# Attention matmuls in a fixed order of one-form blocks, and conditioning in four column groups summed by way of DRAM

## The chip, the core and the metric

The kernel runs on one core of a Trainium2 chip. TensorE (PE) multiplies, VectorE (DVE) and ScalarE (ACT) do the elementwise work, GpSimd (POOL) and SyncE (SP) issue transfers. The metric is the device time of one execution in microseconds, the median of several runs. Every time below comes from the profile, the runs or the trace of this kernel.

## What is computed

Two transformer blocks in sequence on 512 tokens of width 1024, float32. The first block conditions its input on a vector, attends over a neighbourhood and a context, mixes with a gated unit, and ends in a mixture of 16 experts; the second block has two layers. The change touches the first block's conditioning and attention:

```python
def _adaln(cond, w, b):
    return jnp.split(jax.nn.silu(cond) @ w + b, N_MOD, axis=-1)

# first block
sh_a, sc_a, g_a, sh_f, sc_f, g_f = _adaln(c, w_ada[i], b_ada[i])
csh_a, csc_a, ... = _adaln(c_ctx, w_ada[i], b_ada[i])
h = _modulate(x, sh_a[:, None], sc_a[:, None])
q, k, v, u, vs = _project(h, w_in[i], q_gain[i], k_gain[i])
o_na = _neighborhood_attention(q, k, v, kc, vc, rpb[i])   # softmax(q k + bias) v, 8 heads of 64
o_sg = _sgu(u, vs, sgu_ln[i], sgu_w[i], sgu_b[i])         # gelu(u) * (w_s . layernorm(gelu(vs)) + b_s)
x = x + g_a[:, None] * _merge(o_na, o_sg, out_gain[i], w_out[i])
hf = _modulate(x, sh_f[:, None], sc_f[:, None])
x = x + g_f[:, None] * _hier_moe(hf, ...)
```

## The kernel before

The program is written with a planner: it gets instructions with priorities, and itself fixes their order on each engine and the waits between engines. Most products use a split of the operands into a high and a low part and three matmuls (`mm3`, lines 195 to 197); the attention's transposes and value products and all of the conditioning are plain float32, where each 512-column matmul is two records in the trace.

**Conditioning.** `w_ada` is 1024 x 6144, cut into twelve chunks of 512 columns, each two loads of 1 MB. `ada_row` (line 247) multiplies a chunk: eight matmuls, one for each 128 rows of the weight, whose stationary operand `cst` is 64 columns wide (two of them are the two conditions, the rest zero). Even and odd ones write to rows 0 to 63 and 64 to 127 of one PSUM tile (line 263), so a chunk leaves two partial sums. The copy `row` (line 265) goes on to another matmul that adds the two. For the first four chunks, ahead of the projections, that is line 336, which also turns the row into columns (scale and shift of the attention's input). For the other eight, `ada_store` (line 269) adds the partial sums and the bias with a matmul of one output column (`adab`, line 274) and stores the row in `ada_dram`; the rest of the block reads it back as four broadcasts (`g_a`, `sh_f`, `sc_f`, `g_f`, line 835).

**Attention.** In `first_attention` (line 314), after the projections of q, k, v, vs and u, sixteen steps (m, t): four pairs of heads by four tiles of 128 queries. `scores` (from line 486) makes twelve matmuls of 64 rows, two heads side by side, into two PSUM tiles `sc`; DVE adds the bias and takes the maximum (line 503), ACT takes the exponent (line 227 is the helper), DVE the reciprocal and the scaling (line 512). `values` transposes the probabilities (line 522, eight transposes), copies the first head's with ACT and the second's with DVE (lines 525, 527), and makes eight matmuls with 64 columns (line 531) into `o`. Scores run two steps ahead of values. `sgu_norm`, `sgu_mix` and the eight stores stand in a list `fill`; one of them is put into two steps of three. `sgu_out` (the gate's four transposed tiles) comes at step 13. PSUM has four buffers for scores, two for transposes, one for `o` and one, `any`, for all else. `tc.high_priority` gives scores and values a priority, and the planner puts the matmuls of the fill between them as it sees room. After the steps, the squares of the attention's output are summed (line 578), the rows are normalised, and `first_rest` (line 824) makes the output projection, the gate's half of the rows first.

Of the kernel before, what the change touches and what calls it, by code (L numbers as in the profile page):

```python
# [14 lines left out]
P = 128  # L15
# [3 lines left out]
ND = 512  # L19
# [19 lines left out]
C_SEL = 640  # L39
# [229 lines left out]
def ada_store(c, cst, j, dst):  # L269

    nc = c.nc
    row = ada_row(c, cst, j, c.a["b_ada"][j - 4:j - 3, :])
    ps = c.ps("adab")
    nc.tensor.matmul(ps[0:1, :], c.k[0:97, C_SEL:C_SEL + 1], row[0:97, :], start=True, stop=True)
    out = c.t("adao")
    nc.scalar.copy(out[0:1, :], ps[0:1, :])
    nc.gpsimd.dma_start(dst, out[0:1, :])
# [36 lines left out]
def first_attention(c, x, cst, v_dram, ada_dram):  # L314

    nc, tc, a = c.nc, c.tc, c.a
    with ExitStack() as st:
# [13 lines left out]
        with tc.tile_pool(name="early", bufs=6, reuse_waits="tile") as early, tc.issue_after(xload.ins):  # L331
            c.more_raws((early, "raw", 6), own_first=True)
            for j in range(4):
                row = ada_row(c, cst, j)
                for q in range(4):
                    nc.tensor.matmul(pc[:, (j * 4 + q) * 2:(j * 4 + q) * 2 + 2], row[0:66, q * P:(q + 1) * P],
                                     c.k[0:66, C_SEL2:C_SEL2 + 2], start=True, stop=True)
# [119 lines left out]
        def sgu_mix():  # L457
            sgw = R3.tile([P, 8, P], F32, name="sgw", tag="b8")
            nc.gpsimd.dma_start(sgw, a["sgu_w"])
            for g in range(8):  # L460
                po = c.ps("mix")[:, :256].rearrange("p (n d) -> p n d", n=4)
                nc.tensor.matmul(po, sgw[:, g], vn[:, :, g * 64:(g + 1) * 64], start=True, stop=True)
                go = gate[:, :, g * 64:(g + 1) * 64]
                nc.vector.scalar_tensor_tensor(go, po, c.vecs[:, 10 + g:11 + g], go, op0=OP.add, op1=OP.mult)
            ss = R.tile([P, 4], F32, name="ss")
# [4 lines left out]
            for i in range(4):  # L470
                nc.vector.tensor_scalar_mul(gate[:, i], gate[:, i], ss[:, i:i + 1])

        def sgu_out():
            held["y1"] = [c.xs.tile([P, 4, 512], F32R, name="y1", tag="xs") for _ in range(2)]
            for m in range(4):
                ps = c.ps("gT")
                for i in range(4):
                    nc.tensor.transpose(ps[:, i * P:(i + 1) * P], gate[:, i, m * P:(m + 1) * P], c.ident)
                y = c.t("ysg")
                nc.vector.tensor_scalar_mul(y, ps, og[:, 4 + m:5 + m])  # L480
                c.split(held["y1"][0][:, m], held["y1"][1][:, m], y)

        store = lambda j: ada_store(c, cst, j, ada_dram[j - 4:j - 3, :])
        on = []

        def scores(m, t):
            w = WIN0[t]
            sc = [c.ps("sc") for _ in range(2)]
            for part in range(2):
                for step in range(3):  # L490
                    for e in range(2):
# [6 lines left out]
                        nc.tensor.matmul(sc[e][:, part * 256:part * 256 + 256], q, k, start=step == 0, stop=step == 2)  # L498
# [16 lines left out]
        def values(m, t, prob):  # L515
            if t == 0:
                held["o"] = c.ps("o")
            pt = []
            for e in range(2):
                pT = c.ps("pT")  # L520
                for j in range(4):
                    nc.tensor.transpose(pT[:, j * P:(j + 1) * P], prob[e][:, j * P:(j + 1) * P], c.ident)
                pt.append(c.t("pt"))
                if e == 0:
                    nc.scalar.copy(pt[e], pT)
                else:
                    nc.vector.tensor_copy(pt[e], pT)
            for j in range(4):
                v = vw[:, t, j] if j < 2 else vc[:, j - 2]
                for e in range(2):  # L530
                    nc.tensor.matmul(held["o"][e * 64:e * 64 + 64, t * P:(t + 1) * P], v[:, m * P + e * 64:m * P + e * 64 + 64],
                                     pt[e][:, j * P:(j + 1) * P], start=j == 0, stop=j == 3)
            if t == 3:
                on.append(RQ.tile([P, S], F32, name="on", tag="q"))
                nc.scalar.copy(on[m].rearrange("p (r t c) -> p t r c", r=8, t=4),
                               held["o"].rearrange("p (t r c) -> p t r c", t=4, r=8))

# [36 lines left out]
        msq = c.ps("msq")  # L574
        for m in range(4):
# [1015 lines left out]
```

## Time and profile before

| what | us |
|---|---|
| median of three runs (2596.69 to 2597.25) | 2596.92 |
| the profiled execution | 2599.29 |
| its span | 2597.5 |
| PE busy in the span | 2493.9 (96%) |
| DVE busy | 1414.4 (54%) |
| ACT busy | 1058.5 (41%) |

The profile shows one execution. A timeline row has start, duration, engine, line, operation, tiles (out<-in), the array's rows*columns in use, the shape and, in brackets, idle time of the engine before it. A duration has the matmul's way through the array in it, so successive starts tell the pace. A group row has count, busy time, mean duration and the idle time before. The granted clock is a share of 2.4 GHz.

### The profile page before, as it was taken

How to read it: one execution, taken by the hardware profiler on the slowest of the kernel's cores; microseconds unless marked ns; L12 is line 12 of the kernel's file. 1: busy time of each engine (PE TensorE's matmuls, PEld its weight loads, DVE VectorE, ACT ScalarE, POOL GpSimd, SP SyncE). 2: the span in 40 equal slices, each digit the busy share in tenths (PEclk: the TensorE clock that was granted, in tenths of full speed). 3: DMA queues.
4: the chain of work that ended last, by engine and by line, in shares of the span. 5: the costliest groups of instructions: out<-in, count | busy, mean ns of one | idle time of the engine just before them, and what ended most of it. 6: DMA issues, size and time to landing. Idle time of an engine off the chain costs nothing.

```text
span 2597.5 us, 30968 instructions
## 1 busy us (share of the span) xinstructions
PE 2493.9 (96%) x12305; PEld 2024.4 (78%) x12305; DVE 1414.4 (54%) x2393; ACT 1058.5 (41%) x1632; POOL 90.2 (3%) x111
## 2 busy tenths in 40 slices
PE   7999986999999999999999999999999999999997
PEld 3785455888888888887788888888888877888886
DVE  3735355999963333369963333443333699633334
ACT  3523232888842222254652232342222546522222
POOL 0011001121100000000000000000000000000000
PEclk9999987999999999999999999999999999999999
DMA  6243365999932222331122222322222311222231
GB/s 259 82 126 122 130 245 215 358 396 391 389 129 83 97 97 85 105 118 70 66 69 96 98 92 89 110 97 96 94 89 96 118 65 66 82 98 98 77 105 61
DMA packets 59524, 347.98 MB, mean 134 GB/s; under 512 B 8832, under 2 KB 11040, under 8 KB 23280
## 3 DMA queue, kind: packets, MB, share of 16 engines
q1 hardware_dynamic: 47776, 311.45, 32.8%
q0 software_dynamic: 10448, 31.86, 4.2%
q10 hardware_dynamic: 1152, 2.66, 0.3%
q8 instruction: 97, 1.59, 0.3%
q14 instruction: 51, 0.42, 0.0%
HBM read 329.67 MB, written 16.27 MB: 133 GB/s over the span
## 4 chain that ended last, share of the span: by engine, by line
PE 70%; DVE 9%; ACT 4%; issue 1%; ACTq 0%; another core or an unknown queue 0%; DVEq 0%
PE t L195 12%; PE t L196 12%; PE t L197 12%; PE y L195 7%; PE y L197 7%; PE y L196 7%; PE e L195 2%; PE e L197 2%; PE e L196 2%; DVE acc L1222 2%; DVE wl L187 1%; PE ft L195 1%; PE ft L196 1%; PE ft L197 1%; ACT x L1085 1%
## 5 line engine op out<-in xcount | busy, mean ns | idle before, releaser
L186 ACT CAST wh<-raw 128x1024 fp32r<-128x1024 f32 (+1 forms) x504 | 521.5, 1038 | 1077.1 <-PE t L197 350.3
L187 DVE TENSOR_TENSOR wl<-raw,wh 128x1024 fp32r<-128x1024 f32 (+1 forms) x504 | 600.9, 1207 | 605.9 <-ACT wh L186 601.9
L195 PE MATMUL t<-xh,wl 128*128 128x512 f32 x1440 | 562.0, 390 | 0.0
L196 PE MATMUL t<-xl,wh 128*128 128x512 f32 x1440 | 561.2, 390 | 0.0
L197 PE MATMUL t<-xh,wh 128*128 128x512 f32 x1440 | 560.9, 389 | 0.0
L195 PEld LDWEIGHTS t<-xh,wl 128*128 128x128 f32 x1440 | 270.7, 188 | 58.5 <-issue 2.3
L197 PEld LDWEIGHTS t<-xh,wh 128*128 128x128 f32 x1440 | 270.7, 188 | 56.4
L196 PEld LDWEIGHTS t<-xl,wh 128*128 128x128 f32 x1440 | 270.6, 188 | 56.4 <-issue 0.8
L195 PE MATMUL y<-hh,wl 128*128 128x512 f32 (+1 forms) x792 | 289.8, 366 | 2.1 <-DVE x L1049 2.1
L196 PE MATMUL y<-hl,wh 128*128 128x512 f32 (+1 forms) x792 | 290.2, 366 | 0.0
L197 PE MATMUL y<-hh,wh 128*128 128x512 f32 (+1 forms) x792 | 289.4, 365 | 0.0
L1135 DVE SCALAR_TENSOR_TENSOR s<-s,t 128x512 f32<-128x512 f32 x80 | 55.1, 688 | 254.7 <-PE t L197 254.7
L195 PEld LDWEIGHTS y<-hh,wl 128*128 128x128 f32 x792 | 149.3, 189 | 27.0 <-DVE x L1049 2.9
L196 PEld LDWEIGHTS y<-hl,wh 128*128 128x128 f32 x792 | 149.4, 189 | 24.3
L197 PEld LDWEIGHTS y<-hh,wh 128*128 128x128 f32 x792 | 149.4, 189 | 24.1
L195 PE MATMUL ft<-xh,wl 128*128 128x256 f32 x384 | 104.8, 291 | 8.0 <-ACT xh L1090 6.8
L196 PE MATMUL ft<-xl,wh 128*128 128x256 f32 x384 | 110.4, 292 | 0.7 <-DVE xl L1091 0.7
L195 PE MATMUL e<-wh,hTl 128*128 128x512 f32 x272 | 108.3, 398 | 0.5 <-DVE hTl L187 0.5
L197 PE MATMUL ft<-xh,wh 128*128 128x256 f32 x384 | 108.8, 288 | 0.0
L197 PE MATMUL e<-wh,hTh 128*128 128x512 f32 x272 | 106.6, 392 | 0.0
L196 PE MATMUL e<-wl,hTh 128*128 128x512 f32 x272 | 106.4, 391 | 0.0
L1222 DVE SCALAR_TENSOR_TENSOR acc<-yp,hw,acc 128x512 f32<-128x512 f32 x120 | 85.6, 755 | 0.1
(473 smaller groups left out, 3485.7 us busy)
## 6 DMA issues: line engine op xcount, KB each, us to landing
raw<-in_w_gu SPq DMA_DIRECT2D x88, 1024.0 KB, 4.7
raw<-in_w SPq DMA_DIRECT2D x82, 1024.0 KB, 11.4
raw<-in_w_d SPq DMA_DIRECT2D x32, 1024.0 KB, 4.9
raw<-in_w_ada SPq DMA_DIRECT2D x24, 1024.0 KB, 4.9
pair<-in_w SPq DMA_DIRECT2D x14, 1024.0 KB, 12.5
raw<-in_w_in SPq DMA_DIRECT2D x14, 1024.0 KB, 4.7
raw<-in_w_out SPq DMA_DIRECT2D x12, 1024.0 KB, 4.7
raw<-in_w_d SPq DMA_DIRECT2D x32, 384.0 KB, 3.1
```

The lines of the kernel that those rows point to most:

```text
L186: self.nc.scalar.copy(h, x)
L187: self.nc.vector.tensor_sub(l, x, h.bitcast(F32))
L195: mm(ps, al, bh, start=first, stop=False)
L196: mm(ps, ah, bl, start=False, stop=False)
L197: mm(ps, ah, bh, start=False, stop=last)
L1085: nc.scalar.activation(r, t, AF.Identity, bias=b[:, d:d + 1], scale=g[:, d:d + 1])
L1135: nc.vector.scalar_tensor_tensor(s, s, 0.5, ps[1], op0=OP.mult, op1=OP.mult)
L1222: nc.vector.scalar_tensor_tensor(acc[:, t], yp[:, t, j:j + S], w, acc[:, t], op0=OP.mult, op1=OP.add)
```

## The change

In attention, the matmuls are kept in program order (`pin`). A step is written as: the extra work of the step (mixing in steps 1 to 4, the gate's tiles in 7 to 10, three of four square sums in 14), the transposes, the scores of the step after next, in eight of the steps one conditioning chunk, then the values. Both copies of the transposes are DVE's; the scaling of the probabilities and of the gate is ACT's. The normalisation of the gate goes among the u projections. In conditioning, `cst` is 32 columns wide and a chunk's matmuls write to four groups of 32 rows, so there are four partial sums. For the eight later chunks these are stored in DRAM; after every fourth chunk the sums of four are read back in another layout, added on DVE to the bias and stored again. `sc_f` and `sh_f` change places.

```diff
-def ada_row(c, cst, j, bias=None):
+def ada_row(c, cst, j, pin=lambda i: i):
-    if bias is not None:
-        nc.gpsimd.memset(row[64:128, :], 0.0)
-        nc.gpsimd.dma_start(row[96:97, :], bias)
         w = [c.load(c.a["w_ada"][j, half], 2048) for half in range(2)]
     for half in range(2):
         for k in range(4):
-            g = slice(k % 2 * 64, k % 2 * 64 + 64)
-            nc.tensor.matmul(ps[g, :], cst[:, half * 4 + k], w[half][:, k * 512:(k + 1) * 512],
-                             start=half == 0 and k < 2, stop=half == 1 and k > 1)
-    nc.scalar.copy(row[0:66, :], ps[0:66, :])
+            pin(nc.tensor.matmul(ps[k * 32:k * 32 + 32, :], cst[:, half * 4 + k], w[half][:, k * 512:(k + 1) * 512],
+                                 start=half == 0, stop=half == 1))
+    nc.scalar.copy(row[0:98, :], ps[0:98, :])
...
+class Condition:
+    ORDER = (4, 5, 8, 9, 6, 7, 10, 11)
...
+    def chunk(self, n, pin):
+        c, nc = self.c, self.c.nc
+        row = ada_row(c, self.cst, self.ORDER[n], pin)
+        nc.gpsimd.dma_start(self.sums[n], row[0:97:32, :])
+        if n % 4 == 3:
+            part = n // 4
+            t, out = c.t("sums"), c.t("rows")[0:16, 0:P]
+            nc.gpsimd.dma_start(out, c.a["b_ada"][part])
+            for q in range(4):
+                nc.gpsimd.dma_start(t[q * 4:q * 4 + 4, :].rearrange("q (a p) -> q a p", a=4),
+                                    self.sums[part * 4 + q].rearrange("a (q p) -> q a p", p=P))
+            for a in range(4):
+                nc.vector.tensor_add(out, out, t[0:16, a * P:(a + 1) * P])
+            nc.gpsimd.dma_start(self.dst[part].rearrange("r (q p) -> (r q) p", p=P), out)
...
-        def sgu_mix():
+        def sgu_mix(g2):
...
+            ps = c.ps("mix")
+            for g in range(2 * g2, 2 * g2 + 2):
+                po = ps[:, g % 2 * 256:g % 2 * 256 + 256].rearrange("p (n d) -> p n d", n=4)
+                pin(nc.tensor.matmul(po, held["sgw"][:, g], vn[:, :, g * 64:(g + 1) * 64], start=True, stop=True))
...
-        def sgu_out():
+        def sgu_out(m):
+            ps = c.ps("gT")
+            for i in range(4):
+                pin(nc.tensor.transpose(ps[:, i * P:(i + 1) * P], gate[:, i, m * P:(m + 1) * P], c.ident))
+            h, l = held["y1"][0][:, m], held["y1"][1][:, m]
+            nc.scalar.mul(h, ps, og[:, 4 + m:5 + m])
+            nc.vector.scalar_tensor_tensor(l, ps, og[:, 4 + m:5 + m], h.bitcast(F32), op0=OP.mult, op1=OP.subtract)
...
+        pin = tc.keep_in_program_order
...
             for e in range(2):
-                nc.vector.tensor_scalar_mul(prob[e], prob[e], s8[:, 3, e:e + 1])
+                nc.scalar.mul(prob[e], prob[e], s8[:, 3, e:e + 1])
...
+        def turned(prob):
             pt = []
             for e in range(2):
                 pT = c.ps("pT")
                 for j in range(4):
+                    pin(nc.tensor.transpose(pT[:, j * P:(j + 1) * P], prob[e][:, j * P:(j + 1) * P], c.ident))
                 pt.append(c.t("pt"))
-                if e == 0:
-                    nc.scalar.copy(pt[e], pT)
-                else:
-                    nc.vector.tensor_copy(pt[e], pT)
+                nc.vector.tensor_copy(pt[e], pT)
+            return pt
...
+        def squares(m):
+            if m == 0:
+                held["msq"] = c.ps("msq")
+            sq = c.t("osq")
+            nc.scalar.square(sq, on[m])
+            pin(nc.tensor.matmul(held["msq"], c.ones, sq, start=m == 0, stop=m == 3))
...
         for i in range(4):
             u_tile(i)
+            if i == 1:
+                sgu_norm()
         phase.close()
-        fill = [sgu_norm, sgu_mix] + [lambda j=j: store(j) for j in range(4, 12)]
+        cond = Condition(c, cst, sums_dram, ada_dram)
+        extra = {1 + g: [lambda g=g: sgu_mix(g)] for g in range(4)}
+        extra[5] = [sgu_scale]
+        extra.update({7 + m: [lambda m=m: sgu_out(m)] for m in range(4)})
+        extra[14] = [lambda m=m: squares(m) for m in range(3)]
...
-                if j % 3 != 2 and fill:
-                    fill.pop(0)()
-                if j == 13:
-                    sgu_out()
+                for f in extra.get(j, ()):
+                    f()
+                s, prob = ready.pop(0)
+                pt = turned(prob)
                 if j + 2 < 16:
-                    with tc.high_priority(offset=0):
-                        ready.append((steps[j + 2], scores(*steps[j + 2])))
-                s, prob = ready.pop(0)
-                with tc.high_priority(offset=0):
-                    values(*s, prob)
+                    ready.append((steps[j + 2], scores(*steps[j + 2])))
+                if j in (0, 2, 4, 6, 8, 10, 12, 13):
+                    cond.chunk((j + 1) // 2, pin)
+                values(*s, pt)
+            squares(3)
+            rs = c.t("ors")
+            c.rstd(rs, held["msq"], ND, 1e-6)
...
-        for j, n in enumerate(("g_a", "sh_f", "sc_f", "g_f")):
+        for j, n in enumerate(("g_a", "sc_f", "sh_f", "g_f")):
...
-        cst = first.tile([P, KD, 64], F32, name="cst")
+        cst = first.tile([P, KD, 32], F32, name="cst")
```

## Rows read from the trace of the kernel before

**Rows 1.** Table of stretches: length, busy PE, PEld, DVE, ACT, POOL, clock, DMA, GB/s

```profile
150.00:200.00 50.00, 50.00 (x222) 41.01 (x220) 13.22 (x16) 13.57 (x17) 3.84 (x6) 1.00 0.46 130
...
200.00:210.00 10.00, 7.94 (x57) 6.58 (x57) 8.73 (x28) 5.86 (x13) 0.00 (x0) 0.80 0.00 0
...
270.00:280.00 10.00, 10.00 (x37) 4.06 (x35) 0.83 (x2) 1.64 (x3) 1.51 (x3) 1.00 0.00 0
...
340.00:350.00 10.00, 3.84 (x17) 2.81 (x16) 9.27 (x17) 3.80 (x9) 1.06 (x2) 0.50 0.66 222
```

**Rows 2.** Groups by line and form, 200 to 410 us: busy us, mean ns, idle before

```profile
L263 PE MATMUL ada<-raw,cst 128*64 128x512 f32 x128 | 48.8, 608 | 0.4 <-DVE gate L464 0.3
...
L227 ACT ACTIVATE ring<-sc,s 128x512 f32<-128x512 f32 x32 | 21.7, 681 | 18.0 <-DVE s L505 17.9
L503 DVE CUSTOM_DVE_ANT_1 sc<-sc,bias 128x512 f32<-128x512 f32 x24 | 16.3, 707 | 27.8 <-PE sc L498 27.6
...
L527 DVE COPY pt<-pT 128x512 f32<-128x512 f32 x16 | 11.1, 691 | 58.2 <-PE pT L522 43.6 <-issue 14.6
...
L274 PE MATMUL adab<-row,consts 97*1 97x512 f32 x16 | 8.2, 590 | 0.0
L227 ACT ACTIVATION_READ_ACCUMULATOR ring<-sc,s 128x1 f32 x32 | 6.3, 196 | 0.0
...
L503 DVE DVE_READ_ACCUMULATOR2_ANT s<- 128x1 f32 x32 | 4.6, 142 | 0.0
...
L186 ACT CAST y<-ysg 128x512 fp32r<-128x512 f32 x4 | 2.5, 622 | 5.8 <-DVE ysg L480 5.8
```

**Rows 3.** Timeline of PE, transposes and conditioning in alternation

```profile
245.88 0.33 PE L522 MATMUL pT<-consts,ring 128*128 128x128 f32 x1
246.14 1.07 PE L263 MATMUL ada<-raw,cst 128*64 128x512 f32 x2
247.15 0.33 PE L522 MATMUL pT<-consts,ring 128*128 128x128 f32 x1
```

**Rows 4.** Timeline of PE, unbroken blocks

```profile
227.86 1.09 PE L522 MATMUL pT<-consts,ring 128*128 128x128 f32 x8
...
292.49 3.65 PE L263 MATMUL ada<-raw,cst 128*64 128x512 f32 x16
295.98 0.38 PE L531 MATMUL o<-pt,vw 128*64 128x128 f32 x2
```

**Rows 5.** Timeline of PE, start of the attention steps

```profile
199.93 0.39 PE L498 MATMUL sc<-kh,ql 64*128 64x256 f32 x2
...
200.74 0.28 PE L498 MATMUL sc<-kh,ql 64*128 64x256 f32 x2
...
205.99 1.97 PE L522 MATMUL pT<-consts,ring 128*128 128x128 f32 x8
```

**Rows 6.** Timeline of PE, end of the attention and first output matmul

```profile
355.92 3.70 PE L578 MATMUL msq<-osq,consts 128*128 128x512 f32 x8
362.51 0.50 PE L195 MATMUL wo<-wh,y 128*128 128x512 f32 x1 [2.89 <-DVE rs L211]
```

**Rows 7.** Timeline of PE, conditioning ahead of the projections

```profile
19.29 3.65 PE L263 MATMUL ada<-raw,cst 128*64 128x512 f32 x16
...
35.33 3.66 PE L263 MATMUL ada<-raw,cst 128*64 128x512 f32 x16
39.66 1.05 PE L336 MATMUL cols<-consts,row 66*128 66x2 f32 x8 [0.68 <-ACT row L265]
```

**Rows 8.** The tile of the early weight loads: issues, and time to landing

```profile
L139 SPq DMA_DIRECT2D raw<-in_w_ada x8: 328/376/671, 1.6 to 15.5; - x8
...
DMA to landing us min/median/max: 11.3/12.6/13.4
```

**Rows 9.** Transfers issued 190 to 380 us: count, KB, median us to landing

```profile
raw<-in_w_ada SPq DMA_DIRECT2D x14, 1024.0 KB, 4.7
...
ada_dram<-adao POOLq DMA_DIRECT2D x8, 2.0 KB, 2.2
```

More of the change, by code (lines that the diff above doesn't have):

```diff
@@ L261, in ada_row, with __init__ @@
         for k in range(4):
-            g = slice(k % 2 * 64, k % 2 * 64 + 64)
-            nc.tensor.matmul(ps[g, :], cst[:, half * 4 + k], w[half][:, k * 512:(k + 1) * 512],
-                             start=half == 0 and k < 2, stop=half == 1 and k > 1)
-    nc.scalar.copy(row[0:66, :], ps[0:66, :])
-    return row
[L269 to L277, printed above, removed]
+            pin(nc.tensor.matmul(ps[k * 32:k * 32 + 32, :], cst[:, half * 4 + k], w[half][:, k * 512:(k + 1) * 512],
+                                 start=half == 0, stop=half == 1))
+    nc.scalar.copy(row[0:98, :], ps[0:98, :])
+    return row
+class Condition:
+    ORDER = (4, 5, 8, 9, 6, 7, 10, 11)
+    def __init__(self, c, cst, sums_dram, rows_dram):
+        self.c, self.cst, self.sums, self.dst = c, cst, sums_dram, rows_dram
+    def chunk(self, n, pin):
[12 more added lines that the diff above has]
+            nc.gpsimd.dma_start(self.dst[part].rearrange("r (q p) -> (r q) p", p=P), out)
 def rms_in(c, x, n):
@@ L335, in first_attention @@
                 for q in range(4):
-                    nc.tensor.matmul(pc[:, (j * 4 + q) * 2:(j * 4 + q) * 2 + 2], row[0:66, q * P:(q + 1) * P],
-                                     c.k[0:66, C_SEL2:C_SEL2 + 2], start=True, stop=True)
+                    nc.tensor.matmul(pc[:, (j * 4 + q) * 2:(j * 4 + q) * 2 + 2], row[0:98, q * P:(q + 1) * P],
+                                     c.k[0:98, C_SEL2:C_SEL2 + 2], start=True, stop=True)
             bias = c.vecs[:, V_ADA:V_ADA + 16].unsqueeze(2).to_broadcast([P, 16, 2])
@@ L455, in sgu_norm, with sgu_scale @@
                 nc.vector.tensor_mul(vn[:, i], vn[:, i], lnb)
-        def sgu_mix():
[L458 to L462, printed above, removed]
+        def sgu_mix(g2):
+            if g2 == 0:
+                held["sgw"] = R3.tile([P, 8, P], F32, name="sgw", tag="b8")
+                nc.gpsimd.dma_start(held["sgw"], a["sgu_w"])
+            ps = c.ps("mix")
+            for g in range(2 * g2, 2 * g2 + 2):
+                po = ps[:, g % 2 * 256:g % 2 * 256 + 256].rearrange("p (n d) -> p n d", n=4)
+                pin(nc.tensor.matmul(po, held["sgw"][:, g], vn[:, :, g * 64:(g + 1) * 64], start=True, stop=True))
+            for g in range(2 * g2, 2 * g2 + 2):
+                po = ps[:, g % 2 * 256:g % 2 * 256 + 256].rearrange("p (n d) -> p n d", n=4)
                 go = gate[:, :, g * 64:(g + 1) * 64]
                 nc.vector.scalar_tensor_tensor(go, po, c.vecs[:, 10 + g:11 + g], go, op0=OP.add, op1=OP.mult)
+        def sgu_scale():
             ss = R.tile([P, 4], F32, name="ss")
@@ L470, in sgu_mix @@
             for i in range(4):
-                nc.vector.tensor_scalar_mul(gate[:, i], gate[:, i], ss[:, i:i + 1])
-        def sgu_out():
[L474 to L483, printed above, removed]
+                nc.scalar.mul(gate[:, i], gate[:, i], ss[:, i:i + 1])
+        def sgu_out(m):
+            if m == 0:
+                held["y1"] = [c.xs.tile([P, 4, 512], F32R, name="y1", tag="xs") for _ in range(2)]
+            ps = c.ps("gT")
[5 more added lines that the diff above has]
+        pin = tc.keep_in_program_order
         on = []
@@ L497, in scores @@
                             k = (kch, kcl, kch)[step][pr, m]
-                        nc.tensor.matmul(sc[e][:, part * 256:part * 256 + 256], q, k, start=step == 0, stop=step == 2)
+                        pin(nc.tensor.matmul(sc[e][:, part * 256:part * 256 + 256], q, k, start=step == 0, stop=step == 2))
             s8 = c.cst.tile([P, 4, 2], F32, name="s8", tag="s8", bufs=4)
@@ L530, in values @@
                 for e in range(2):
[L531 to L532 removed]
+                    pin(nc.tensor.matmul(held["o"][e * 64:e * 64 + 64, t * P:(t + 1) * P],
+                                         v[:, m * P + e * 64:m * P + e * 64 + 64],
+                                         pt[e][:, j * P:(j + 1) * P], start=j == 0, stop=j == 3))
             if t == 3:
@@ L1479, in host @@
     b_ada = f("b_ada")[0].reshape(12, 512)[perm]
[L1480 removed]
+    o["b_ada"] = b_ada[list(Condition.ORDER)].reshape(2, 16, P)
     w = f("w_in")[0]
```

31 lines of the change are left out of this document (11 added, 20 removed).

## The prediction

> **What bounds the kernel now.** The busy shares of the page say that TensorE (PE) works nearly all the time, so I went to what fills that time. The table of stretches comes first: in the attention stage PE is busy from end to end (10.00 of 10 us between 270 and 280) while DVE works 0.83 and ACT 1.64 us; near its end PE does 3.84 of 10 us at a granted share of 0.50, which is 1.2 of 2.4 GHz; the start (200 to 210) stands at 0.80 [rows 1]. So PE sets the pace there. Next, whether that work has to cost so much. The timeline shows why not: in the middle of the stage single instructions of different shapes take turns. One transpose and then one conditioning instruction: the transpose goes at 245.88, the conditioning matmul at 246.14, the next transpose at 247.15 [rows 3]. In a block of its own kind the same conditioning work costs far less: 16 records (8 instructions of two) from 292.49 to 295.98, 3.49 us [rows 4], so 0.436 us for an instruction, against 1.01 in the alternation. Two things are lost: 64-column instructions stand side by side in pairs only if they follow each other (one alone takes 0.87), and each turn of shape costs another 0.12 to 0.14 us, which I take as 0.15.
>
> The stage runs from the first score, 199.93 [rows 5], to the first square sum, 355.92 [rows 6]: 156.0 us. In whole blocks its work would be: 8 conditioning chunks x 3.49 = 27.9; 8 bias sums (adab), 8.2 in all [rows 2]; 16 steps of scores at 0.81 (199.93 to 200.74, the next step's first) [rows 5] = 13.0; 16 x 8 transposes at 1.09 [rows 4] = 17.4; 16 value blocks, by an estimate from the chunk's pace (a record of 512 columns 0.218, so of 128 columns 0.055, 16 of them 0.87) = 13.9; the gate's mixing and transposes by the same paces 3.5 + 2.2. Together 86 us. Some 70 us are alternation, waits and the half clock.
>
> **The change, part by part.** *Four column groups.* A chunk keeps 8 matmuls, but four run side by side instead of two. The trace shows that two groups halve the time (3.49 for 8, where one alone costs 0.87). Four are not shown: between no gain (3.49) and a further half (1.74). I take 1.74, because the step from one group to two was whole, and keep 3.49 for the range. The Trainium skill, "TensorE: Matmul & The Clock Gate", section "Measured speedup vs the span model", gives three 32-column tiles as 2.38 times one; carried on to four, an estimate, a chunk would cost 2.2 us and the twelve chunks of the kernel together 5 us more than my sum, and no run here shows it.
>
> *Early conditioning (4 chunks before the projections).* Chunks start at 19.29 and 35.33, three periods of 5.35 us, each 3.49 of matmuls, the rest row copy and column sums; the last sums begin at 39.66 [rows 7]. Less 1.74 each, the fourth chunk would start at 19.29 + 3 x 3.61 = 30.1. Its weights don't hold it up: the last load is issued at 15.5 and lands within 13.4, by 29 [rows 8]. Everything behind follows the column sums: 4 x 1.74 = 7.0 us won, or 0 if four groups are no faster.
>
> *Attention in fixed blocks.* A step is now 8 transposes (1.09), scores of the step after next (0.81 + 0.15), in every second step a chunk (1.74 + 0.15), values (0.87 + 0.15). Sum: 16 x 3.07 = 49.1; 8 x 1.9 = 15.2; mixing 3.5, gate transposes 2.2, three square sums 2.6 (they come before transposes, the same shape). The bias sums leave PE. Total 72.6 us if nothing waits.
>
> *What now waits.* PE's order is fixed, so a late operand holds all that is behind it.
> (1) Start: from the first scores to the first transpose the softmax takes 205.99 - 199.93 = 6.1 us [rows 5]; PE has two score blocks (1.6) and then nothing: 4.4 us. Before, it slipped scores of later steps in there.
> (2) Each step's values wait for both transposes to be copied by DVE, 2 x 0.69 [rows 2], since ACT's copy moves to DVE and the scaling of the probabilities from DVE to ACT. PE has 0.96 of scores to cover 1.4 and perhaps a running reduction (0.71 + 0.14): 0.4 to 1.3 exposed in the 8 steps without a chunk, 0.8 taken, 6.4 us; a chunk covers it in the others.
> (3) One PSUM buffer serves chunks, mixing and gate transposes in turn. In steps 7 to 10 ACT and then DVE empty it in a row (0.62 + 0.7 and their queues); six hand-overs at 1 to 2.5 us, 10 us.
> (4) The chunk of step 13 comes one step after that of 12; a load takes 4.7 us from issue [rows 9] and its buffer comes free only with the former chunk: 3 us.
> (5) Clock: a lull at the start already has the share at 0.80 there [rows 1], and mine is longer: work of about 6 us at half speed, 3 us lost.
> The softmax of a step, 6.1 - 0.8 = 5.3 us, has to fit between its scores and its transposes: values 1.0, transposes 1.1, scores 1.0, a chunk 1.9, values 1.0 make 6.0. It fits, narrowly. DVE needs 2 x 0.85 + 2 x 0.69 = 3.1 us a step, 49 in all; ACT 2 x (0.68 + 0.20) and two scalings, estimated at the 0.62 of an ACT pass of that shape, 3.0 a step, 48 in all, and some 28 passes besides at 0.6, 17 [rows 2]. Both stay under PE's 72.6.
> Stage: 72.6 + 4.4 + 6.4 + 10 + 3 + 3 = 99.4, so 156.0 - 99.4 = 56.6 us won.
>
> *End.* Three of four square sums are made early; output matmuls that need only the gate's half may start behind the last values, where before they waited 6.6 us (355.92 to 362.51) for the normalisation [rows 6]. They have 48 matmuls to cover it. 0.5 us left over: 6.1 won, 0 if their buffers are again those of the square sum.
>
> *Sums by way of DRAM, other moves.* A chunk's four partial rows are stored, read back, added on DVE and stored again: three trips at about 2.2 us [rows 9]; for each half of the rows POOL's queue carries ten instructions, where it had twelve (memset, load and store for each chunk). The first half is complete at step 6, the second at step 13, some 12 us before the stage ends; the second's broadcasts are wanted only after the first output half. Cost 0; if the additions stand at the head of DVE's queue before their data is there, DVE and with it PE waits up to 6 us, twice. The gate's normalisation (eight DVE passes, one broadcast load on POOL's queue, two more loads of ACT's table) goes among the u projections, where in 50 us DVE works 13.22 and ACT 13.57 [rows 1]: 0. On POOL's queue the first half's read-backs stand ahead of the last head pair's bias table (issued at step 8, wanted at 10) and the second half's ahead of the last two broadcasts; both have steps to spare.
>
> Sum: 7.0 + 56.6 + 6.1 = 69.7. The profiled execution took 2599.29 us (span 2597.5), the median of the runs 2596.92, 0.1% apart; I subtract from the median: 2527.
>
> **The rivals.** *Four groups run no faster than two.* Early gain 0; 8 x 1.74 = 13.9 more on PE, of which some 3 fill waits: 2527 + 7 + 11 = 2545. For it: nothing in the trace has four. Against: the whole gain from one to two.
> *The clock stays at 1.2 GHz through the stage*, because PE now rests in every step. 2 x 72.6 + 4.4 = 150 us: 6 won there, 2577 in all. For it: the 0.80 and 0.50 of stretches with lulls [rows 1]. Against: at half speed the work leaves no rests, and full stretches stand at 1.00.
> *Evictions on one engine are the bound.* What the trace shows is that DVE's share of these copies lasts 0.69 us each [rows 2]. If they come behind reductions every time, 0.7 us more is exposed in each step: 16 x 0.7 = 11, 2538. The Trainium skill, "TensorEngine Tiling (Array Packing)", section "PSUM Bottleneck", asks for both engines at this place; the change goes against it.
> *Slower.* The narrow fit fails: softmax of one step no longer runs beside the blocks of others, because DVE's or ACT's queue holds one step's pass behind another's. A step is then 3.07 + 0.95 + 4.4 (chain without scores) + 1.4 (copies) = 9.8 us, 157 in all, and PE, busy 4 of 9.8, falls to 1.2 GHz: 64 more, about 2660 with the rest. It decides from 10.7 us a step, (156 + 13)/16. Against it: 6.0 over 5.3.
> *It doesn't do what it says:* PE's blocks come apart all the same, and the new trips to DRAM cost what is saved: about 2597.
>
> **How the numbers follow.** Forecast 0.66, four groups useless 0.11, low clock 0.08, evictions 0.07, slower 0.05, no effect 0.03. Low end: waits (3) to (5) gone (16 us) and cheaper turns (56 x 0.05 = 3) and some 6 of (2): 2502. High end: the first and third rival together, 2556, and part of the second: 2566. Under 0.2% (5 us) a measurement can't tell from no change; faster 0.92, within it 0.03, slower 0.05.
>
> **What would show it.** Column sums ending at 33 to 35 instead of 40.7; conditioning blocks of about 1.8 us; transposes, scores and values in unbroken blocks; a step of 5 to 6 us; from first score to last value 90 to 110 us; output matmuls within 1 us of the last value; the rest of the kernel unchanged in length. Wrong would be: chunks still 3.5 us, the share of the clock near 0.5 over the stage, PE waiting for DVE's copies by more than 1.5 us a step, DVE waiting for loads from the sums.

## The result, and the profile after

| | before | after |
|---|---|---|
| median, us (4 runs each) | 2597.09 | 2530.78 |
| lowest to highest | 2596.69 to 2597.93 | 2528.66 to 2532.05 |
| span of the profiled execution | 2597.5 | 2529.0 |
| first score to last value, starts, us | 199.93 to 355.72 | 193.06 to 288.71 |
| last column sum, starts | 40.46 | 33.13 |
| first output matmul, starts | 362.51 | 291.30 |
| last output matmul, starts | 419.84 | 351.44 |

The ratio is 0.9742, 95% interval 0.973 to 0.9754: 66 us faster, where 2527 was forecast. The rows below follow the order of the sum. All are of the changed kernel unless a sentence names another.

Stretches (length; busy PE, PEld, DVE, ACT, POOL; granted clock; DMA; GB/s):

```profile
193.00:289.00 96.00, 79.83 (x743) 54.51 (x742) 59.32 (x157) 64.34 (x134) 14.29 (x28) 0.93 0.57 210
193.00:203.00 10.00, 5.91 (x49) 4.61 (x52) 5.25 (x15) 7.33 (x14) 0.00 (x0) 0.76 0.00 0
233.00:243.00 10.00, 8.08 (x73) 5.76 (x70) 3.83 (x14) 8.39 (x19) 1.78 (x4) 0.84 0.56 209
243.00:253.00 10.00, 9.88 (x96) 7.25 (x95) 7.79 (x21) 5.94 (x14) 1.91 (x4) 0.85 0.35 118
289.00:300.00 11.00, 9.68 (x34) 7.19 (x35) 1.81 (x3) 2.53 (x4) 5.64 (x10) 0.84 0.96 390
```

The stage is 96 us, and PE works 79.8 of them. It was 156 with PE busy from end to end in the middle [rows 1]. The share of the clock is 0.93: parts of the stage run at 1.2 instead of 2.4 GHz, the start among them, after a lull.

PE's conditioning group in the stage (busy us, mean ns, idle before and its releaser):

```profile
L258 PE MATMUL ada<-raw,cst 128*32 128x512 f32 x128 | 17.0, 645 | 2.7 <-DMA raw<-in_w_ada 2.5
```

The same 128 records, 17.0 us of PE where there were 48.8 [rows 2].

PE's timeline, first the early chunks, then the first transposes, a step in blocks, and the end of the stage:

```profile
18.86 1.92 PE L258 MATMUL ada<-raw,cst 128*32 128x512 f32 x16
22.47 1.92 PE L258 MATMUL ada<-raw,cst 128*32 128x512 f32 x16
...
32.33 1.05 PE L345 MATMUL cols<-consts,row 98*128 98x2 f32 x8 [0.70 <-ACT row L260]
...
198.84 1.97 PE L535 MATMUL pT<-consts,ring 128*128 128x128 f32 x8 [4.09 <-ACT ring L527]
...
213.72 1.93 PE L258 MATMUL ada<-raw,cst 128*32 128x512 f32 x16
215.57 0.66 PE L546 MATMUL o<-pt,vw 128*64 128x128 f32 x8
...
290.32 1.97 PE L559 MATMUL msq<-osq,consts 128*128 128x512 f32 x2 [1.34 <-ACT osq L558]
291.30 1.41 PE L194 MATMUL wo<-wh,y 128*128 128x512 f32 x1
```

A chunk is now 1.85 us from its start to the next kind of work (213.72 to 215.57), where the block of before took 3.49 [rows 4]; the early chunks follow each other after 3.61 us, not 5.35 [rows 7]. Counted over the whole stage, PE's work turns from one kind to another (conditioning, bias sum, score, value, and transposes with all full-width work) 54 times; in the kernel before it was 240 times.

PE's waits in the stage (us, times, longest):

```profile
PE o L546 <- DVE pt L537: 6.1, 7, 2.0
PE pT L535 <- ACT ring L527: 4.1, 1, 4.1
PE ada L258 <- DMA raw<-in_w_ada: 2.5, 2, 1.4
PE gT L493 <- ACT row L260: 1.9, 1, 1.9
PE mix L473 <- ACT row L260: 1.1, 1, 1.1
```

### The profile page after: what moved, and what is told of

It is laid out like the page before. It is cut to its first block, busy times and chain, and to the rows that moved or that the text cites. A ratio compares the mean times of both kernels' runs of the same rounds, so it can differ in the third digit from the quotient of the medians.

```text
span 2529.0 us, 30912 instructions
## 1 busy us (share of the span) xinstructions
PE 2416.5 (96%) x12289; PEld 1998.9 (79%) x12289; DVE 1405.1 (56%) x2373; ACT 1073.7 (42%) x1650; POOL 89.2 (4%) x107
## 4 chain that ended last, share of the span: by engine, by line
PE 72%; DVE 9%; ACT 4%; issue 1%; DMA 0%; DVEq 0%; another core or an unknown queue 0%; ACTq 0%
PE t L194 12%; PE t L196 12%; PE t L195 12%; PE y L194 7%; PE y L196 7%; PE y L195 7%; PE e L194 2%; PE e L196 2%; PE e L195 2%; DVE acc L1246 2%; DVE wl L186 1%; PE ft L194 1%; PE ft L195 1%; PE ft L196 1%; ACT x L1109 1%
```

## The experiments

Times are medians; each kernel ran beside the kernel before, at 2598.0 to 2599.1 in these runs, so ratios are what is compared. "Stage" is from the start of the first score to that of the last value.

| kernel | us | ratio, 95% interval | stage, us | turns of kind |
|---|---|---|---|---|
| before | 2597.09 | 1 | 155.8 | 240 |
| after | 2530.78 | 0.9742 (0.973, 0.9754) | 95.6 | 54 |
| planner_order: after, no hold in program order | 2520.76 | 0.9704 (0.9688, 0.972) | 85.6 | 83 |
| planner_priority: the same, with the priority of before | 2590.24 | 0.9965 (0.9952, 0.9978) | 161.8 | 303 |
| before_no_priority: before, without the priority | 2565.88 | 0.9878 (0.9863, 0.9893) | 125.2 | 117 |
| before_four_groups: before, four groups | 2578.99 | 0.9931 (0.9914, 0.9947) | 145.2 | 216 |
| before_both: before, both of these | 2558.29 | 0.9848 (0.9832, 0.9865) | 124.7 | 110 |
| two_groups: after, two groups | 2542.66 | 0.9791 (0.9775, 0.9807) | 104.0 | 54 |
| both_copy: after, copies on both engines | 2531.7 | 0.9746 (0.973, 0.9762) | 94.9 | 54 |
| sums_on_pe: after, sums on TensorE | 2538.88 | 0.977 (0.9756, 0.9783) | 111.1 | 62 |
| one_early: after, the 1 added early | 2523.98 | 0.9715 (0.9702, 0.9728) | 95.6 | 54 |
| chunk_first: after, a chunk ahead of the steps | 2524.31 | 0.9711 (0.9698, 0.9724) | 97.6 | 54 |
| both: the last two edits together | 2527.53 | 0.9721 (0.9708, 0.9734) | 97.8 | 54 |
| planner_one: no hold, the 1 added early | 2515.25 | 0.9676 (0.9663, 0.969) | 86.3 | 86 |

### What makes the blocks

**The hold taken away.**

```diff
-        pin = tc.keep_in_program_order
+        pin = lambda i: i
```

> The changed kernel, but the matmuls of the stage are not held in program order; the planner places them. Four groups, sums by way of DRAM and the moves between ACT and DVE stay. If the alternation of shapes is what cost the old stage its 70 us, PE's timeline falls apart again into single instructions and most of the 50 us of the stage return: 2570 to 2585. If the gain is in fewer and better spread operations, under 10 us return: 2531 to 2541.

Measured 2520.76: 10 us faster than with the hold. My theory, that the hold makes the blocks, fell, and the rival's 2531 to 2541 was missed as well. The planner alone leaves 83 turns, not 240, and does better than the fixed order. Which way the 10 us go shows in the stretches of the two stages; of this kernel:

```profile
192.40:278.20 85.80, 81.03 (x743) 52.68 (x742) 56.79 (x151) 63.98 (x134) 14.84 (x29) 1.00 0.60 222
```

PE is busy 81.0 us, 1.2 more than with the hold (79.8), but at full clock, and rests 4.8 us instead of 16.2. With the hold, the granted share of 0.93 means 0.07 x 96 = 6.7 us of full clock withheld. So its work at full clock is some 73 us, 8 less than without it, and it pays 11.4 more in rests and 6.7 in clock. That is how the 10.2 us between the two stages divide.

**The priority put back.** In the kernel before, scores and values stood under a priority (`tc.high_priority`, described with the attention loop ahead of the prediction); the change drops it when it rewrites that loop, and the prediction gave this no term. This kernel has no hold and gives the priority back to transposes, scores and values.

```diff
-        pin = tc.keep_in_program_order
+        pin = lambda i: i
...
-                pt = turned(prob)
+                with tc.high_priority(offset=0):
+                    pt = turned(prob)
                 if j + 2 < 16:
-                    ready.append((steps[j + 2], scores(*steps[j + 2])))
+                    with tc.high_priority(offset=0):
+                        ready.append((steps[j + 2], scores(*steps[j + 2])))
...
-                values(*s, pt)
+                with tc.high_priority(offset=0):
+                    values(*s, pt)
```

> The changed kernel without the hold, and with the priority of the kernel before given to transposes, scores and values (not to chunks, mixing and gate tiles). Theory: in the kernel before it was this priority that put single transposes, score and value matmuls between those of the chunks, since the favoured work takes every free slot and what is not favoured fills the gaps one instruction at a time; then this kernel alternates again: over 150 turns of shape in the stage where the one without hold and priority has 84, the stage 25 to 45 us longer, 2545 to 2565. Rival: the order in which a step is written and the four groups carry the gain, and the priority changes little: 2518 to 2530.

Measured 2590.24, slower than the theory's 2545 to 2565: nearly the whole gain is gone. The stretch of its stage, its conditioning group, and a piece of its timeline:

```profile
194.40:356.50 162.10, 155.62 (x743) 71.31 (x742) 60.42 (x157) 64.32 (x134) 16.07 (x31) 0.98 0.39 136
```

```profile
L258 PE MATMUL ada<-raw,cst 128*32 128x512 f32 x128 | 54.2, 604 | 0.0
```

```profile
255.99 0.33 PE L535 MATMUL pT<-consts,ring 128*128 128x128 f32 x1
256.25 1.04 PE L258 MATMUL ada<-raw,cst 128*32 128x512 f32 x2
257.22 0.33 PE L535 MATMUL pT<-consts,ring 128*128 128x128 f32 x1
257.48 1.04 PE L258 MATMUL ada<-raw,cst 128*32 128x512 f32 x2
```

This is the alternation of before [rows 3], with four column groups in place. PE does the same instructions as the kernel above and needs 155.6 us for them instead of 81.0. It hardly waits (6.5 us), and its clock is granted at 0.98: the loss is in how the work is cut up. The conditioning group alone goes from 18.1 us in planner_order to 54.2, since one conditioning instruction by itself (two records) takes 0.97 us of PE (256.25 to 257.22) with 32 columns, about what it took with 64, 1.01 [rows 3].

**The kernel before without the priority.**

```diff
                 if j + 2 < 16:
-                    with tc.high_priority(offset=0):
-                        ready.append((steps[j + 2], scores(*steps[j + 2])))
+                    ready.append((steps[j + 2], scores(*steps[j + 2])))
                 s, prob = ready.pop(0)
-                with tc.high_priority(offset=0):
-                    values(*s, prob)
+                values(*s, prob)
```

> The kernel before with the priority of scores and values taken away and nothing else. Theory (the priority makes the alternation): the conditioning chunks go in whole blocks, 8 x (8 x 1.01 - 3.49) = 36 us at most come back, some of it is lost to waits since nothing else is reordered: 2560 to 2580, and fewer than 150 turns of shape in the stage. Rival (the written order makes it): within 10 us of the kernel before, 2588 to 2608.

Measured 2565.88, 32.7 less than before in the same runs, within the theory's range. Its stage and its conditioning group:

```profile
198.40:323.80 125.40, 112.91 (x753) 68.25 (x752) 70.19 (x186) 53.82 (x121) 17.55 (x35) 0.90 0.49 177
```

```profile
L263 PE MATMUL ada<-raw,cst 128*64 128x512 f32 x128 | 36.6, 598 | 0.2
```

So two kernels, old writing and new, agree: with the priority PE's work comes apart, without it there are less than half as many turns, and nobody has to hold it. Whether a hold would make the blocks with the priority still in place was not run. What it costs depends on the writing: 33 us in the old, 69 in the new.

### Four column groups

**The changed kernel with two groups**, in the form of the kernel before (64 columns, groups at 0 and 64, two partial sums to store and add).

```diff
-            pin(nc.tensor.matmul(ps[k * 32:k * 32 + 32, :], cst[:, half * 4 + k], w[half][:, k * 512:(k + 1) * 512],
-                                 start=half == 0, stop=half == 1))
+            g = slice(k % 2 * 64, k % 2 * 64 + 64)
+            pin(nc.tensor.matmul(ps[g, :], cst[:, half * 4 + k], w[half][:, k * 512:(k + 1) * 512],
+                                 start=half == 0 and k < 2, stop=half == 1 and k > 1))
...
```

> The changed kernel with two column groups of 64 in place of four of 32 in all twelve chunks; order, sums by way of DRAM and all else as changed. If four groups side by side save what the sum says (1.74 us a chunk), the early chunks lose 7.0 and the stage 8 x 1.74 less what fills waits, 11: 2530.8 + 18 = 2549. If the fixed order alone makes the gain and PE's rests in the stage swallow the longer chunks, the stage loses under 3: 2541.

Measured 2542.66, 12 us above the changed kernel and between the two expectations. The early part loses what it had won (last column sum 39.63, not 33.13), and the stage is 8.4 us longer, not 13.9:

```profile
198.70:302.90 104.20, 88.86 (x743) 59.06 (x742) 58.44 (x153) 64.45 (x134) 15.21 (x30) 0.97 0.54 194
```

PE is busy 9.0 us more and rests 0.9 less. The rests hardly cover the longer chunks: waits for the value operands fall to 3.2 us from 6.1, but those for the gate's and the mixing's buffer grow to 5.7 from 3.0. More than half of what is missing from 13.9 is the clock, granted at 0.97 instead of 0.93, some 3 us withheld instead of 6.7; why it fell less was not tested.

**The kernel before with four groups and no other edit** (the same four lines as in the change, with a 99-row selection for the bias sum).

> The kernel before, with four column groups alone: chunks in four groups, the four partial sums and the bias added by the same one-column matmul. The planner's order stays. The early chunks win 7.0. In the stage, if alternation rules, an instruction that stands alone costs 1.0 us whether 64 or 32 columns wide; only chunks in blocks gain, so 0 to 8 of the possible 14: 2582 to 2590. If the chunk's own work ruled, all 14: 2576. A much larger gain would speak against alternation.

Measured 2578.99, 19.6 less, in between once more. The early part wins 7.4 us and the stage 10.6. Its conditioning group shows why not more, and why not nothing:

```profile
L262 PE MATMUL ada<-raw,cst 128*32 128x512 f32 x128 | 37.4, 603 | 0.5 <-DVE gate L463 0.3
```

48.8 became 37.4: whole blocks are halved, single instructions between others are not.

**Both edits in the kernel before: four groups and no priority.**

> The kernel before with two parts and nothing else: the priority of scores and values taken away, and four column groups for all twelve chunks (bias sums stay on TensorE). Alone the first gave 33 us and the second 19.6 us. Theory: they take different time (turns of shape, and the length of a chunk), the sum is 52.3 and the time 2546, the rest of the change (its other writing, the bias sums off TensorE) is then worth 25 us, down to the 2520.8 of the changed kernel without hold. Rival: four groups pay more in whole blocks, where all 16 records lie side by side (the chunks of the stage took 36.6 us without the priority and take 18.5 in the best kernel, 18 less, and 7 early): 25 us from 2566, so 2541 or below.

Measured 2558.29, and both expectations fell: beside before_no_priority only the early 7 us are won, and the stage does not shrink (124.7 against 125.2).

```profile
192.50:317.40 124.90, 109.89 (x753) 62.11 (x752) 71.55 (x186) 53.18 (x121) 17.66 (x35) 0.88 0.48 178
```

```profile
L262 PE MATMUL ada<-raw,cst 128*32 128x512 f32 x128 | 26.7, 639 | 0.0
L273 PE MATMUL adab<-row,consts 99*1 99x512 f32 x16 | 8.2, 590 | 2.8 <-DMA row<-in_b_ada 1.6 <-ACT row L264 1.2
```

Conditioning takes 9.9 us less of PE (36.6 to 26.7), but PE as a whole is busy only 3.0 less and rests 2.5 more. The scores' groups, laid out anew by the planner, take 4.8 more (45.3 to 50.1 in the sum of their six groups), bias sums wait 1.8 us longer, and the clock is granted at 0.88 instead of 0.90; how much of the 4.8 is the lower clock was not separated. The remaining 39 us between this stage and the 85.6 of planner_order are the rest of the new writing: sums off PE (below), the gate's work ahead of the stage and in pieces, the scaling on ACT. Only the first was tried by itself, in the held order; it made 15.5 us of stage there, so some 24 of the 39 have no part of the change shown for them. One place shows in the trace of before_both:

```profile
295.00:317.40 22.40, 13.93 (x82) 8.88 (x82) 12.89 (x17) 8.67 (x13) 2.10 (x4) 0.70 0.63 247
```

PE rests 8.5 us here, most of them for the gate's transposes, which wait for DVE, and some 6.7 us of clock are withheld. In the changed kernel the gate's tiles stand in steps 7 to 10. That this is what they win was not tested.

### Copies on both engines

**ACT copies the first head's transposes again, and DVE scales the probabilities.**

```diff
                 pt.append(c.t("pt"))
-                nc.vector.tensor_copy(pt[e], pT)
+                if e == 0:
+                    nc.scalar.copy(pt[e], pT)
+                else:
+                    nc.vector.tensor_copy(pt[e], pT)
...
-                nc.scalar.mul(prob[e], prob[e], s8[:, 3, e:e + 1])
+                nc.vector.tensor_scalar_mul(prob[e], prob[e], s8[:, 3, e:e + 1])
```

> The changed kernel, but the transposes of the first head are copied by ACT and those of the second by DVE, and DVE scales the probabilities, as before the change. If two copies in a row on DVE are what PE's values wait for (6.1 us in the changed kernel's trace), most of that goes: 2525 to 2528. If the passes only change engines and the scaling now stands between DVE's reductions, the softmax gets no shorter and the waits move from the values to the transposes: 2529 to 2537.

Measured 2531.7, no difference from the changed kernel. PE's waits in the stage only change their name:

```profile
PE o L549 <- ACT pt L538: 4.2, 5, 2.5
PE pT L535 <- DVE ring L527: 3.4, 1, 3.4
...
PE o L549 <- DVE pt L540: 2.6, 3, 0.9
```

4.2 + 2.6 in the place of 6.1. Both engines serve one chain per step, and moving a pass from one to the other moves the wait with it. A small gain may be hidden: the stage is 0.7 us shorter, but the output matmuls then wait 4.2 us for `y`, not 2.2 (the wait of the next part).

### The sums by way of DRAM

**Sums on TensorE again, in the held order.** Each chunk's four partial rows and the bias are added by a one-column matmul after the step's values, and the row is stored.

```diff
-        nc.gpsimd.dma_start(self.sums[n], row[0:97:32, :])
-        if n % 4 == 3:
...
+    def sum(self, pin):
...
+        ps = c.ps("adab")
+        pin(nc.tensor.matmul(ps[0:1, :], c.k[0:99, C_SEL:C_SEL + 1], self.row[0:99, :], start=True, stop=True))
+        out = c.t("adao")
+        nc.scalar.copy(out[0:1, :], ps[0:1, :])
+        nc.gpsimd.dma_start(self.dst[n // 4][n % 4:n % 4 + 1, :], out[0:1, :])
...
```

> The changed kernel, but the four partial sums of the eight later chunks and the bias are added by a one-column matmul behind the step's values, as in the kernel before; nothing goes by way of DRAM but the finished row. Price by the sum: 8 x (0.87 + 0.15) = 8 us more on PE and a further hand-over of the one PSUM buffer, less the tail's wait for the broadcasts (3 to 5): 2534 to 2540. If the way by DRAM costs more than it saves, this one is faster than 2530.

Measured 2538.88, as expected: the way through DRAM is worth 8 us net. The group says where they are:

```profile
L286 PE MATMUL adab<-row,consts 99*1 99x512 f32 x16 | 8.2, 594 | 9.2 <-ACT row L261 9.2
```

8.2 us of matmuls and 9.2 of waiting for the row's copy; the stage is 15.5 us longer. In the kernel before the same sums waited for nothing [rows 2], so the 9.2 belong to their place right behind the step's values, and another place was not tried. About half comes back after the stage, because the output matmuls are then not held up as follows.

**Where the way through DRAM costs time.** In the changed kernel the first output matmul is 71.2 us earlier than before (362.51 to 291.30), the last only 68.4 (419.84 to 351.44). POOL and then DVE after the last values:

```profile
288.64 0.53 POOL L286 DMA_DIRECT2D ada_dram<-rows  x1 [5.68 <-DVE cum L691]
289.16 0.59 POOL L859 DMA_DIRECT2D g_a<-ada_dram  x1
289.75 0.53 POOL L859 DMA_DIRECT2D sc_f<-ada_dram  x1
```

```profile
302.09 0.69 DVE L860 TENSOR_SCALAR sc_f<-sc_f 128x1024 f32<-128x1024 f32 x1 [6.50 <-DMA sc_f<-ada_dram]
302.70 0.68 DVE L212 TENSOR_TENSOR ors<-rs,rs 128x512 f32<-128x512 f32 x1
303.42 0.75 DVE L607 SCALAR_TENSOR_TENSOR yna<-on,vecs,ors 128x512 f32<-128x512 f32 x1
```

The rows of `sc_f` are complete since the first half, but their broadcast stands on POOL's queue behind the store of the second half, which waits for DVE's additions. It is issued at 289.75 and takes 12.3 us to land. On DVE, `sc_f` plus 1 stands ahead of the attention's normalisation, so that waits 6.5 us for a number that is needed much later. PE has the first half of the output matmuls to do meanwhile and rests 2.2 us ahead of the second:

```profile
306.15 0.50 PE L194 MATMUL wo<-wh,y 128*128 128x512 f32 x1 [2.18 <-DVE y L186]
```

**The 1 added to the 16 rows of sums**, ahead of the additions, so that no DVE pass waits for the broadcast.

```diff
+            if part == 0:
+                nc.vector.tensor_scalar(out, out, c.k[0:16, C_SCF:C_SCF + 1], None, op0=OP.add)
             for a in range(4):
                 nc.vector.tensor_add(out, out, t[0:16, a * P:(a + 1) * P])
...
-        nc.vector.tensor_scalar_add(bcs["sc_f"], bcs["sc_f"], 1.0)
...
```

> The changed kernel, but the one that is added to the scale of the second modulation is added to the 16 x 128 rows of the sums, ahead of the store, and not by DVE to the broadcast. In the changed kernel that pass waits 6.5 us at the head of DVE's queue for the broadcast, and the normalised rows behind it come late: PE rests 2.2 us and works 3.4 us at half the clock. If that is what is lost after the stage, output matmuls run through and the whole gains 3 to 5: 2526 to 2528. If the normalised rows are late for another reason, no gain: 2530 to 2532.

Measured 2523.98, 6.8 less, where 3 to 5 were expected. DVE goes on with the normalisation at once:

```profile
295.11 0.43 DVE L212 TENSOR_SCALAR rs<-rs 128x512 f32<-128x512 f32 x1
295.57 0.69 DVE L213 TENSOR_TENSOR ors<-rs,rs 128x512 f32<-128x512 f32 x1
```

The last output matmul starts 4.7 us earlier than in the changed kernel, the first expert's 6.1.

### The lull at the start

**Chunk 0 goes ahead of the steps, the others one step later.**

```diff
+            cond.chunk(0, pin)
             for j, (m, t) in enumerate(steps):
...
-                if j in (0, 2, 4, 6, 8, 10, 12, 13):
+                if j in (1, 3, 5, 7, 9, 11, 13):
```

> The changed kernel, but the first chunk of the stage stands ahead of the steps, right behind the first two score blocks, and the others in every odd step up to 13. PE's first lull (4.1 us) then holds a chunk of 1.9 us, and no chunk follows another after one step, so the wait for a load (2.5 us) goes. Theory: 1.9 + 2.5 = 4.4 less, 2526. Rival: the lull is the softmax's, the later steps keep its pace, and the chunk that covered the first values' wait is missed: 0 to 2 less, 2529 to 2531.

Measured 2524.31, 6.5 us less, but not for the reason given. PE's waits in its stage:

```profile
PE gT L493 <- ACT row L260: 6.6, 2, 5.4
PE o L546 <- DVE pt L537: 5.1, 4, 2.6
...
PE pT L535 <- ACT ring L527: 2.2, 1, 2.2
```

The lull shrinks from 4.1 to 2.2 us, as meant, and the waits for loads are gone, but the gate's transposes now wait 6.6 us for the one PSUM buffer, not 1.9, and the stage is 2 us longer. The 5.4 of them start on DVE:

```profile
244.24 0.28 DVE L285 TENSOR_TENSOR rows<-rows,sums 16x128 f32<-16x128 f32 x1 [4.68 <-DMA sums<-sums_dram]
244.69 0.69 ACT L226 ACTIVATE ring<-sc,s 128x512 f32<-128x512 f32 x1 [6.32 <-DVE s L520]
```

The first addition of the sums stands at the head of DVE's queue before they are read back. The softmax on ACT waits for DVE, and the copy of the row that frees the buffer stands behind it on ACT. The gain comes after the stage. The broadcast of `sc_f` lands 5.1 us after its issue, not 12.3, before DVE comes to it; why it is quicker was not tested. The wait for `y` among the output matmuls is absent, as in one_early: from first to last output matmul it takes 54.2 us, not 60.1 (347.26 - 293.07, 351.44 - 291.30).

**Both edits at once.**

> Both former edits together, one added early and the first chunk ahead. If they work at different places their gains add: 2521 to 2524. If the one pulls the other's wait along, the better of the two alone: 2526.

Measured 2527.53, with an interval that overlaps those of either alone: the gains do not add, since both remove the same wait. The stage keeps its extra 2 us. Here the pass that adds the 1 stands at the head of DVE's queue ahead of its data:

```profile
238.59 0.28 DVE L286 TENSOR_SCALAR rows<-rows,consts 16x128 f32<-16x128 f32 x1 [3.81 <-DMA rows<-in_b_ada]
```

In that step PE rests 4.4 us before its chunk.

### The best version

**No hold, and the 1 added early.**

> The changed kernel without the hold in program order (the planner places the matmuls) and with sc_f's 1 added to the 16 rows of sums instead of to the broadcast. Theory: the two costs lie in different places (the hold's waits in the attention stage, the addition at the head of DVE's queue behind the last values), so the gains add up to what is exposed: without the hold the output matmuls still wait 3.8 us for DVE's y, so 2520.8 less 3.8 or a little more, 2515 to 2518. Rival: they do not add, as the chunk ahead of the steps and the early 1 did not; 2520 to 2524, with PE's wait for y replaced by one for something else.

Measured 2515.25, the theory's case; a ratio of 0.9676 (0.9663 to 0.969) against 0.9742 (0.973 to 0.9754) of the changed kernel. Stage, conditioning group and waits:

```profile
193.70:280.40 86.70, 81.69 (x743) 52.17 (x742) 56.83 (x152) 64.15 (x135) 14.98 (x29) 1.00 0.60 220
```

```profile
L259 PE MATMUL ada<-raw,cst 128*32 128x512 f32 x128 | 18.5, 602 | 1.1 <-DMA raw<-in_w_ada 0.7 <-DVE y L499 0.2
```

```profile
PE o L549 <- DVE pt L540: 1.1, 4, 0.4
PE sc L516 <- ACT ring L227: 1.0, 1, 1.0
PE ada L259 <- DMA raw<-in_w_ada: 0.7, 1, 0.7
```

## Why the prediction was right, and where it was not

The time lay 4 us from the forecast. The size of the gain was read rightly; one cause was not, and terms were off in opposite directions.

*What bounds the kernel:* right. PE was busy with the turns themselves. planner_priority repeats it most plainly: the same instructions, 155.6 us of PE instead of 81.0. The duration of one conditioning instruction in the alternation, 1.01 us, against 0.436 in its block [rows 3, 4] was the right pair of numbers to build on.

*What removes the turns:* wrong. The prediction took the hold in program order as the cause and passed over the dropped priority. The held order has the fewest turns (54), but the hold is not needed (2520.76 without it) and costs 10 us. The priority alone brings back 69 us in the new writing and is worth 33 in the old one. The kernel's description had the fact: the planner puts the rest of the matmuls between those with a priority. The step that failed is that a dropped line of the diff was given no term. That the blocks came as forecast is in part luck: what is shown to make them was in the change, but not in the argument.

*Four groups:* right. Four run side by side: the early period fell by 5.35 - 3.61 = 1.74, and 4 x 1.74 = 7.0 is what the first score gained (199.93 to 193.06, 6.9). The estimate from the Trainium skill, "TensorE: Matmul & The Clock Gate", section "Measured speedup vs the span model", 2.2 us a chunk from 2.38 for three tiles, is not borne out here: a chunk took 1.85 with the turn behind it, some 1.7 without. The 0.87 for an instruction alone, on which the step from one group to two rested, was twice the pace of a pair and not a row; planner_priority shows 0.97 for one with its turns. The rival "no faster than two" is answered by two_groups (2542.66, forecast 2545).

*The stage:* forecast 99.4, measured 96 by the same bounds. Term by term: the work, 72.6, was some 73 at full clock; the start lull 4.4 was 4.1; the values' waits 6.4 were 6.1; step 13's chunk 3 was 2.5. The values' sum came out, but as seven waits of up to 2.0 us and not eight of 0.8. The hand-overs of the one buffer, 10, were 3.0 (gate transposes 1.9, mixing 1.1): mostly the buffer came free in time, since transposes and scores stand between a step's mixing or gate tile and its chunk. The clock, 3, was 6.7: besides the lull at the start, which was foreseen and withheld some 3.5 us (0.76 and then 0.89 in its 20 us), the share fell twice more in the middle (0.84 between 233 and 243, where PE was busy 8.08 of 10 us, and 0.85 in the 10 us behind, where it was busy 9.88). The rival with the low clock all through the stage did not come; the narrow fit of the softmax held.

*The end:* 0.5 us was forecast between last value and first output matmul; it took 2.6 (288.71 to 291.30), 1.34 of it a wait for ACT's square. 4.2 won instead of 6.1.

*The way through DRAM:* cost 0 was forecast, with DVE's additions as the thing to watch. They were not late in this kernel; in chunk_first and in the kernel `both`, DVE did wait at the head of its queue, 4.7 us for a read-back and 3.8 for the bias rows, as the prediction had feared. Here it was the 1 added to `sc_f`, one step further down the same route, that stood 6.5 us at the head of DVE's queue; one_early puts its price at 6.8 us. The prediction had looked at who needs the broadcasts' data, and not at what stands behind them on the queues. It had said that POOL's queue has steps to spare: true of the bias tables, not of the first half's two broadcasts.

*The gate's normalisation among the u projections:* 0, as forecast. From the last column sum to the first score it is 159.5 us before and 159.9 after, with PE busy throughout the last 69 in both.

*Slips in the rivals' sums:* (156 + 13)/16 is 10.6 and not 10.7, the low clock comes to 2578 and not 2577, and the slower case, with the 13 us won elsewhere, to about 2650 and not 2660. None bears on the forecast.

*Evictions on one engine:* 0.07 was given to 2538. The Trainium skill, "TensorEngine Tiling (Array Packing)", section "PSUM Bottleneck", speaks for both engines; both_copy shows 2531.7 against 2530.78, no difference here, with the reserve said there.

Together: 6.9 early + 60.2 in the stage (155.8 - 95.6) + 4.2 at its end - 2.8 among the output matmuls = 68.5, the difference of the two spans. The medians differ by 66.3, since the profiled execution of before was 2 us above its median. So the forecast came out within 4 us partly by luck: a hand-over term that was 7 too large stood against a clock term 3.7 too small, an end that won 1.9 less and a DRAM term of 0 that was 2.8.

## What to carry to other kernels

When work of different shapes can be interleaved on TensorE, look at how the timeline orders it and at what gave it that order, before forcing one: here a priority on the urgent work cut the rest into single instructions, dropping it was worth 33 to 69 us, and a fixed order on top cost 10. Read the deleted lines of a diff as carefully as the added ones, each with a term in the sum. A result that goes by way of DRAM is free only if no instruction that waits for it stands ahead of urgent work in its engine's queue, even one needed much later.

## What was not expected of the hardware

Four column groups of 32 halved the time of two when their instructions stood together (1.85 us for 16 records of 512 columns, two groups 3.49), and gave next to nothing when each stood alone: 0.97 us for one instruction of 32 columns between transposes, 1.01 for one of 64. And rests on PE can be paid for twice: with 16 us of them in 96 the granted clock was 0.93, and the 6.7 us withheld came on top of the 16; with 5 in 87 it was 1.00. But the sum of the rests does not tell the clock: two_groups rested 15 us in 104 at 0.97, chunk_first 20 in 98 at 0.95, before_both 15 in 125 at 0.88. What does was not tested.
